# A two-layer decoder trunk on one core: evacuating transposes bank by bank, and holding weight splits back at three transitions

## The chip, the core and the metric

The kernel runs on one core of a Trainium2 chip. The engines named here are PE (matrix products and transposes), ACT and DVE (both read the accumulator memory PSUM as well as SBUF), POOL, and SP, which here issues the loads of weights. The metric is the device time of one execution in microseconds (us). A profiled execution gives its own time and, beside it, a span from the first to the last recorded instruction; the times quoted from the trace count from the start of the span.

## The reference

One sequence of 256 tokens with 1024 features passes two layers. Everything is float32.

```
h = h + stick_breaking_attention(rms_norm(h, g00), w_qkv, w_o)      # layer 0
h = h + sqrelu_mlp(rms_norm(h, g01), w1[0], w2[0])                  # (relu(x @ w1)^2) @ w2, width 4096
shared = nsa_shared_kv(h, kv_norm, w_kv, cmp_pos, cmp_w1, cmp_w2)   # K and V for three branches
h = h + nsa_attention(rms_norm(h, g10), w_q, gate_b, w_o, shared)   # layer 1: compressed, selected, window
h = h + sqrelu_mlp(rms_norm(h, g11), w1[1], w2[1])
return rms_norm(h, final_norm)
```

Both attentions have 16 heads of 64; in layer 1 three sigmoid gates per head weigh the branches.

## The kernel before

**Products.** A float32 operand is split into a rounded part (hi) and the rest (lo), and a product is taken as hi*hi + hi*lo + lo*hi (`mm3`; all matmuls stand in one helper, L346, all transposes in another, L358). A weight block of 128 x 2048 is loaded by SP into one of three buffers `raw` (L260), in two halves cast by ACT into `wh` (L292) and subtracted by DVE into `wl` (L298); `wh` and `wl` have three buffers too. When the second half's subtraction has been written down, the `raw` buffer is asked for again (`fetch`), which puts the next load on SP.

**Turning the tokens.** `hres` holds the residual stream of two token tiles (128 tokens each). Before an MLP and before layer 1's projections it is transposed: eight chunks of 128 features, four at a time. `xt_tr` puts four chunks into two PSUM banks, two to a bank (eight transposes, tile `pt`), and `xt_evac` takes each out: ACT scales it by the norm's gain (hi, L416), DVE multiplies again and subtracts hi (lo, L417). The results are called `xn` before an MLP and `xk` or `xq` in layer 1. Of the chunks, `2j + b` lies in bank `b` at place `j`: neighbouring chunks lie in different banks. The first four go ahead of the residual's last half, which is added meanwhile (L441 behind attention, L443 behind an MLP), the next four follow.

**Three transitions.** At the end of layer 0 and of layer 1 the output projection (`acc<-wh,oT`) ends, the residual is added, and the MLP's first matmuls (`pu<-xn,wh`) begin; between the first MLP and layer 1 the same happens in `to_nsa`, with `pk<-wh,xk` behind it. DVE and ACT split the following blocks' weights at the same time.

**Layer 1's attention.** For each pair of heads the scores become probabilities `pe` (exponential on ACT, L1058; row sums and gates `rs`; a multiply on DVE, L1086, or POOL, L1085). `turn(p, i, bank)` transposes a third of a pair's `pe` into a bank (tile `ptp`), and ACT or DVE copies it to `pT` (L1111). `values(g, bank)` multiplies by V into a bank (tile `po`), and `part(n, k)` adds a chunk of the output projection (tile `acc`).

**What sets the order.** The instructions of each engine are written out in a fixed order when the program is built, by a planner (`Order`). PE's order is the order of the code. The work of ACT, DVE and POOL stands in chains with a rank, and at each planned moment the free engine takes the ready instruction of the lowest rank; where a form for two engines exists, the one that is free takes it. Residual adds have rank 0.2, evacuations 0.5, splits of the block that PE is at 0.5, of the next block 2, of later ones 4. When PE comes to need a chain, its rank is set to 0. `quiet(engines, ns)` keeps an engine from taking work of rank 2 and above for a planned time. The planner's costs are estimates that only set the order; on the chip each engine takes its list in order and waits where it must.

Of the kernel before, what the change touches and what calls it, by code (L numbers as in the profile page):

```python
# [17 lines left out]
T = 2  # L18
# [153 lines left out]
def hybrid_kernel(ctx, tc, x, xt, eye, gcols, gfin, wqk, wv, wo0, wkv, wvs, wq, wg, wo1, w1, w2, cw1, cw2, cpos, gate_b, consts, out):  # L172
# [10 lines left out]
    def go(gen, rank=1, lag=LAG):  # L183
        return Chain(o, gen, rank, o.now + lag)
# [172 lines left out]
    def tr(o_, a, i, rate=2.0):  # L357
        nc.tensor.transpose(o_, a, i)  # L358
        o.tick(a.shape[0] / 2.4 * rate + 3)
# [42 lines left out]
    def xt_banks(banks):  # L402
        return [B(banks[b], f"pt{b}").rearrange("p (j q) -> p j q", j=2) for b in range(2)]

    def xt_tr(pt, half, ts=range(T)):
        for b in range(2):
            for j in range(2):
                k = 4 * half + 2 * j + b
                for t in ts:
                    tr(pt[b][:, j, t * P:(t + 1) * P], hres[t][:, k * P:(k + 1) * P], ident)  # L410

    def xt_evac(pt, half, gi, xt_, rank=0.5):
        def one(j, b):
            k = 4 * half + 2 * j + b
            g = gc[:, gi * NK + k:gi * NK + k + 1]
            yield act(256, lambda: nc.scalar.activation(xt_[0][:, k, :], pt[b][:, j, :], AF.Copy, scale=g), 60)  # L416
            yield dve(256, lambda: nc.vector.scalar_tensor_tensor(  # L417
                xt_[1][:, k, :], pt[b][:, j, :], g, f32(xt_[0][:, k, :]), op0=OP.mult, op1=OP.subtract), 60)
        return [go(one(j, b), rank) for j in range(2) for b in range(2)]

    def x_tiles(i, tag):
        xp = wide_slot(i, [P, NK, 2, T * P], F32R, f"x{tag}")
# [32 lines left out]
    def mlp(layer, gi, x_, ch, pt, rs, pus, accs, mid, ap):  # L455

        wa, wb = i_m[layer]
        acc = [[None, None], [None, None]]
        held = []
        r2 = [None, None]  # L460

        def second(c, hT, order, hook=None):
            for i, (t, n) in enumerate(order):
                for f in range(2):
                    w = W(wb[c], f)
                    if i == 0 and f == 0:
                        o.need(hT[2])
                    if c == 0 and f == 0:
                        acc[n][t] = B(accs[2 * n + t], f"acc{t}{n}")
                    mm3(acc[n][t], tok(hT, f, t), cut(w, f * D + n * 512, f * D + (n + 1) * 512),  # L470
                        c == 0 and f == 0, c == NFC - 1 and f == 1)
                if hook is not None:
                    hook(i, t, n)
            gone(wb[c])

        by_n = [(t, n) for n in range(2) for t in range(T)]
        by_t = [(t, n) for t in range(T) for n in range(2)]

        def begin(c):
            return ([B(pus[c % 2][f], f"pu{f}") for f in range(2)],  # L480
                    [ap.tile([P, 512], F32, name=m) for m in ("mr", "mu", "ms")], [])

        def first(c, st, f, k0, k1):
            pu, (r, u, s), chains = st
            for part in range(2):
                for k in range(k0, k1):
                    w = W(wa[c], k // 4)
                    if c < 2 and part == 0:
                        o.need(ch[k])
                    a = cut(w, k * 256 + f * P, k * 256 + (f + 1) * P)  # L490
                    if part == 0:
                        mm(pu[f], a[0], x_[2][:, k, :, :], k == 0, False)
                    else:
                        mm(pu[f][:, 0:T * P], a[1], x_[0][:, k, :], False, k == NK - 1)
            if k1 == NK:
                q = slice(f * 256, (f + 1) * 256)

                def gen():
                    yield act(256, lambda: nc.scalar.copy(r[:, q], pu[f][:, 256:512]))  # L499
                    yield dve(256, lambda: nc.vector.tensor_add(u[:, q], pu[f][:, 0:256], r[:, q]))  # L500
                chains.append(go(gen(), 0.4))

        def square(st):
            r, u, s = st[1]
            hh = ap.tile([P, 2, T * P], F32R, name="hh", bufs=3)
            hl = ap.tile([P, 2, T * P], F32R, name="hl", bufs=3)
            sv = s.rearrange("p (f q) -> p f q", f=2)

            def gen():
                for c in st[2]:  # L510
                    yield c
                yield dve(512, lambda: nc.vector.scalar_tensor_tensor(s, u, 0.0, u, op0=OP.max, op1=OP.mult), port=True)  # L512
                yield act(512, lambda: nc.scalar.copy(hh, sv))  # L513
                yield dve(512, lambda: nc.vector.tensor_sub(hl, sv, f32(hh)), port=True)  # L514
            return hh, hl, go(gen(), 0.4)

        st = [begin(0)]
        for f in range(2):
            first(0, st[0], f, 0, NK // 2)
        o.need(*rs)  # L520
        xt_tr(pt, 1)
        ch.extend(xt_evac(pt, 1, gi, x_))
        st.append(begin(1))
        for f in range(2):
            first(1, st[1], f, 0, NK // 2)
        for c in range(2):
            for f in range(2):
                first(c, st[c], f, NK // 2, NK)
            gone(wa[c])
            held.append((c, square(st[c])))  # L530
        for c in range(2, NFC):
            if c in (5, 7):
                go(inverse_of((c - 5) // 2, r2), 3)
            st = begin(c)
            for f in range(2):
                first(c, st, f, 0, NK)
            gone(wa[c])
            held.append((c, square(st)))
            second(*held.pop(0), by_n)
        second(*held.pop(0), by_n)  # L540

        def hook(i, t, n):
            mid(i, go(res(n, t, acc[n][t], r2[t]), 0.2))

        second(*held.pop(0), by_t if layer else by_n, hook)
# [3 lines left out]
    def layer0(ap):  # L549
# [209 lines left out]
        out_part(oT, acc, i_o0, 0, (6, 7), oc[3:4])  # L759
        gone(i_o0[1][0])  # L760
        rs = [go(res(0, t, acc[0][t]), 0.2) for t in range(T)]
        out_part(oT, acc, i_o0, 1, (5,))
        out_part(oT, acc, i_o0, 1, (6,), ts=(0,))
        x1 = x_tiles(0, "n")
        pt = xt_banks((6, 7))
        o.need(*rs)
        xt_tr(pt, 0)
        ch = xt_evac(pt, 0, 1, x1)
        out_part(oT, acc, i_o0, 1, (6,), ts=(1,))
        out_part(oT, acc, i_o0, 1, (7,), ts=(0,))  # L770
        rs = [go(res(1, 0, acc[1][0]), 0.2)]
# [7 lines left out]
    def layer1(xk, pt0, ch, ap):  # L779
# [63 lines left out]
        def kv_proj(n, banks, mid=None):  # L843
            pk = [B(b, "pk") for b in banks]
            for k in range(NK):
                if k == 4 and mid is not None:
                    mid()
                if n == 0 and k == 2:
                    o.need(nxt[2], nxt[3])
                    pt1 = xt_banks((6, 7))  # L850
                    xt_tr(pt1, 1)
                    ch.extend(xt_evac(pt1, 1, 4, xk))
                    rc.extend([go(rstd_of(t, rstd), 0.8) for t in range(T)])
                    for half in range(2):
                        for c, x in enumerate(xt_evac((pt0, pt1)[half], half, 2, xq, 2.5)):
                            qc[4 * half + c] = x
                w = W(i_kv[n][k // 4], k % 4 // 2)
                if n == 0:
                    o.need(ch[k])
                for t in range(T):  # L860
                    mm3(pk[t], tok(xk, k, t), cut(w, k % 4 * 512, (k % 4 + 1) * 512), k == 0, k == NK - 1)
                if k % 4 == 3:
                    gone(i_kv[n][k // 4])
            o.need(*rc)
            for t in range(T):
                if n == 0:
                    kd0c.append(go(first_out(t, pk[t])))
                else:
                    krope[t] = go(key_out(t, pk[t]), 0.9)
# [377 lines left out]
        def part(n, *ks):  # L1247
            out_part(oT, acc, i_o1, n, ks, [oc[k // 2] for k in ks])
# [51 lines left out]
        turn(3, 0, 2)  # L1300
        q_proj(3, 7, 4, 6)
        pcc[0].append(cmp_probs(0, cmp["s0"], 0))
        turn(3, 1, 2)
        q_proj(3, 7, 6, NK)
        turn(3, 2, 1)
        oT = o_tiles(0)
        oc = [None] * NG
        oc[0] = values(0, 0)
# [11 lines left out]
        pcc[1].append(cmp_probs(1, cmp["s1"], 2))  # L1320
        part(0, 2)
        turn(5, 0, 7)
        part(0, 3)
        gone(i_o1[0][0])
        turn(5, 1, 2)
        turn(5, 2, 7)
        oc[2] = values(2, 2)
        scores(7, Z)
# [14 lines left out]
        part(0, 6, 7)  # L1343
        gone(i_o1[1][0])
        rs = [go(res(0, t, acc[0][t]), 0.2) for t in range(T)]
        out_part(oT, acc, i_o1, 1, (6,), ts=(0,))
        x1 = x_tiles(1, "n")
        pt = xt_banks((6, 7))
        o.need(*rs)
        xt_tr(pt, 0)  # L1350
        ch1 = xt_evac(pt, 0, 3, x1)
        out_part(oT, acc, i_o1, 1, (6,), ts=(1,))
        out_part(oT, acc, i_o1, 1, (7,), ts=(0,))
        rs = [go(res(1, 0, acc[1][0]), 0.2)]
# [11 lines left out]

    def to_nsa(i, c):
        nxt[i] = c
        if i == 2:
            nxt["x"] = x_tiles(1, "k")  # L1370
            nxt["pt"] = xt_banks((4, 5))
            o.need(nxt[0], nxt[1])
            xt_tr(nxt["pt"], 0)
            nxt["ch"] = xt_evac(nxt["pt"], 0, 4, nxt["x"])

    scoped(mlp, "m0", 0, 1, x1, ch, pt, rs, ((4, 5), (6, 7)), (0, 1, 2, 3), to_nsa)
    x1, ch, pt, rs = scoped(layer1, "l1", nxt["x"], nxt["pt"], nxt["ch"], bufs=1)
# [128 lines left out]
```

## Time and profile before

| | |
|---|---|
| three runs | 627.76 us median (626.85 to 629.86) |
| profiled execution | 626.71 us, span 624.9 us, TensorE clock granted 0.997 |
| PE busy | 611.7 us, 98% of the span |
| DVE, ACT, POOL busy | 424.4, 328.9, 43.6 us |
| DMA | 108.23 MB, mean 173 GB/s |
| splits on DVE (`wl`, L298) | 192 times, 227.6 us |
| casts on ACT (`wh`, L292) | 192 times, 193.3 us |

The three transitions lie at about 111 to 124 us, 290 to 304 us and 433 to 447 us, layer 1's attention between the second and the third. In the page, a group or a row names the line, the engine, the operation and `out<-in`; an idle time before it is put in brackets with the instruction that ended it. Matmul starts follow each other closer than their lengths, since they are pipelined.

### The profile page before, as it was taken

Reading aid. Unit: us, or ns where it says so; the run is one execution under the profiler, and the core shown is the slowest. Engines: PE = TensorE matmul, PEld = TensorE weight load, DVE = VectorE, ACT = ScalarE, POOL = GpSimd, SP = SyncE. Lnnn points to the kernel's source line nnn. Section 1 sums busy time; section 2 is a strip of 40 time slices with the busy share of each in tenths; the row PEclk is TensorE's granted clock in tenths of the full one; section 3 lists DMA queues with packets and bytes.
Section 4 is the critical chain, followed back from the end, with each engine's and each line's share of the span. In section 5 each row is a group of like instructions: output and inputs, shape, how many; then the busy total and the mean of one; then the engine's idle time right before and its main releaser. Section 6 shows DMA issues by size and latency. Waiting matters only on the chain.

```text
span 624.9 us, 8905 instructions
## 1 busy us (share of the span) xinstructions
PE 611.7 (98%) x3570; PEld 514.2 (82%) x3570; DVE 424.4 (68%) x606; ACT 328.9 (53%) x556; POOL 43.6 (7%) x58
## 2 busy tenths in 40 slices
PE   9999999999999999999999999999999999999995
PEld 6898998788888888887887788677788888888884
DVE  6678896676656666556848999874676665566654
ACT  4756675464545444553815776454554554444432
POOL 0000000000000000000111552330000000000000
PEclk9999999999999999999999999999999999999998
DMA  8964324435554545554455353111455556455501
GB/s 295 393 244 165 113 93 182 149 138 205 194 211 166 195 181 199 202 192 164 174 201 202 137 201 136 69 68 68 168 209 199 200 180 215 162 193 193 203 1 67
DMA packets 17323, 108.23 MB, mean 173 GB/s; under 512 B 2305, under 2 KB 3073, under 8 KB 4993
## 3 DMA queue, kind: packets, MB, share of 16 engines
q1 hardware_dynamic: 16848, 107.11, 47.3%
q8 instruction: 28, 0.46, 0.3%
q10 hardware_dynamic: 432, 0.55, 0.2%
q14 instruction: 15, 0.11, 0.0%
HBM read 106.60 MB, written 1.05 MB: 172 GB/s over the span
## 4 chain that ended last, share of the span: by engine, by line
PE 82%; DVE 10%; DMA 2%; ACT 2%; issue 2%; SPq 0%; POOL 0%; POOLq 0%; ACTq 0%; DVEq 0%
PE acc L346 32%; PE pu L346 28%; PE qk L346 7%; DVE wl L298 4%; PE pk L346 3%; PE po L346 3%; PE z L346 2%; PE pv L346 2%; ACT wh L292 1%; DVE nm L1064 1%; DMA raw<-in_wq 1%; PE qp L346 1%; PE ph L346 1%; DMA raw<-in_wv 1%; PE pa L358 1%
## 5 line engine op out<-in xcount | busy, mean ns | idle before, releaser
L298 DVE TENSOR_TENSOR wl<-raw,wh 128x1024 fp32r<-128x1024 f32 (+1 forms) x192 | 227.6, 1206 | 109.8 <-ACT wh L292 107.4
L292 ACT CAST wh<-raw 128x1024 fp32r<-128x1024 f32 (+1 forms) x192 | 193.3, 1031 | 127.8 <-PE acc L346 54.3
L346 PE MATMUL pu<-xn,wh 128*128 128x512 f32 x512 | 130.1, 392 | 2.0 <-DVE xn L417 1.9
L346 PEld LDWEIGHTS pu<-xn,wh 128*128 128x128 f32 x512 | 93.3, 188 | 20.9 <-DVE xn L417 2.6
L346 PE MATMUL acc<-wh,hh 128*128 128x512 f32 x256 | 100.0, 391 | 0.0
L346 PE MATMUL acc<-wl,hh 128*128 128x512 f32 x256 | 99.9, 390 | 0.0
L346 PE MATMUL acc<-wh,hl 128*128 128x512 f32 x256 | 99.6, 389 | 0.0
L346 PEld LDWEIGHTS pu<-xn,wl 128*128 128x128 f32 x512 | 70.9, 190 | 5.6
L346 PE MATMUL pu<-xn,wl 128*128 128x256 f32 x512 | 72.6, 282 | 0.0
L346 PEld LDWEIGHTS acc<-wh,hl 128*128 128x128 f32 x256 | 48.1, 188 | 10.2
L346 PEld LDWEIGHTS acc<-wh,hh 128*128 128x128 f32 x256 | 48.2, 188 | 9.2
L346 PEld LDWEIGHTS acc<-wl,hh 128*128 128x128 f32 x256 | 48.2, 188 | 8.9
L513 ACT CAST hh<-ms 128x512 fp32r<-128x512 f32 x32 | 19.9, 621 | 61.7 <-DVE ms L512 61.7
L346 PE MATMUL qk<-xa,wh 128*128 128x256 f32 x256 | 47.3, 286 | 0.0
L346 PE MATMUL acc<-wh,oT 128*128 128x512 f32 x128 | 43.6, 403 | 0.0
L346 PEld LDWEIGHTS qk<-xa,wh 128*128 128x128 f32 x256 | 39.8, 191 | 0.5 <-issue 0.3
L346 PE MATMUL qk<-xa,wl 128*128 128x256 f32 x128 | 36.2, 283 | 0.0
L499 ACT COPY mr<-pu 128x256 f32<-128x256 f32 x64 | 23.6, 368 | 22.5 <-PE pu L346 22.5
L514 DVE TENSOR_TENSOR hl<-ms,hh 128x512 fp32r<-128x512 f32 x32 | 22.1, 692 | 19.4 <-ACT hh L513 19.4
L346 PE MATMUL pk<-wh,xk 128*128 128x512 f32 (+1 forms) x128 | 33.6, 342 | 0.0
L1058 ACT ACTIVATE pe<-z,nm 128x256 f32<-128x256 f32 (+1 forms) x64 | 26.1, 429 | 11.6 <-DVE nm L1064 11.4
L500 DVE TENSOR_TENSOR mu<-pu,mr 128x256 f32<-128x256 f32 x64 | 26.6, 418 | 5.2 <-ACT mr L499 5.2
(173 smaller groups left out, 731.6 us busy)
## 6 DMA issues: line engine op xcount, KB each, us to landing
raw<-in_w SPq DMA_DIRECT2D x64, 1024.0 KB, 4.8
raw<-in_wqk SPq DMA_DIRECT2D x8, 1024.0 KB, 7.3
raw<-in_wo SPq DMA_DIRECT2D x8, 1024.0 KB, 4.8
raw<-in_wkv SPq DMA_DIRECT2D x4, 1024.0 KB, 4.8
raw<-in_cw SPq DMA_DIRECT2D x4, 1024.0 KB, 4.8
raw<-in_wq SPq DMA_DIRECT2D x4, 1024.0 KB, 5.1
raw<-in_wv SPq DMA_DIRECT2D x2, 1024.0 KB, 5.8
raw<-in_wvs SPq DMA_DIRECT2D x2, 1024.0 KB, 5.0
```

The costliest lines, as they stand in the source:

```text
L292: nc.scalar.copy(ws.made[j][0][:, r], ws.raws[j][:, r])
L298: nc.vector.tensor_sub(ws.made[j][1][:, r], ws.raws[j][:, r], f32(ws.made[j][0][:, r]))
L346: nc.tensor.matmul(o_, a, b, start=first, stop=last, skip_group_check=True)
L358: nc.tensor.transpose(o_, a, i)
L499: yield act(256, lambda: nc.scalar.copy(r[:, q], pu[f][:, 256:512]))
L500: yield dve(256, lambda: nc.vector.tensor_add(u[:, q], pu[f][:, 0:256], r[:, q]))
L513: yield act(512, lambda: nc.scalar.copy(hh, sv))
L514: yield dve(512, lambda: nc.vector.tensor_sub(hl, sv, f32(hh)), port=True)
L1058: return act(n, lambda: nc.scalar.activation(d, z, AF.Exp, bias=nm[:, i:i + 1], accum_out=rs[:, t, hd, b:b + 1]), 150)
L1064: yield dve(256 * (t + 1), lambda: nc.vector.tensor_reduce(nm[:, i:i + 2], z, axis=AX.X, op=OP.max, negate=True))
```

## The change

Three things are edited. First, transposing and evacuating become one function, `xt_turn`: neighbouring chunks now lie in the same bank (`2b + j`), and the evacuations of a bank are put to the planner as soon as its four transposes stand in PE's list. Second, `quiet` is called at three transitions: for DVE and ACT over a planned 4500 ns at both transitions from attention to MLP, and for DVE over 1500 ns at each of the three calls of `to_nsa` with `i` below 3. Third, in layer 1 two turns exchange their banks (`turn(3,1)` now 1, `turn(3,2)` now 2), and `turn(5,1,2)` stands ahead of `part(0,3)`.

```diff
-    def xt_tr(pt, half, ts=range(T)):
-        for b in range(2):
-            for j in range(2):
-                k = 4 * half + 2 * j + b
-                for t in ts:
-                    tr(pt[b][:, j, t * P:(t + 1) * P], hres[t][:, k * P:(k + 1) * P], ident)
-
-    def xt_evac(pt, half, gi, xt_, rank=0.5):
-        def one(j, b):
-            k = 4 * half + 2 * j + b
-            g = gc[:, gi * NK + k:gi * NK + k + 1]
+    def xt_evac(pt, j, b, half, gi, xt_, rank=0.5):
+        k = 4 * half + 2 * b + j
+        g = gc[:, gi * NK + k:gi * NK + k + 1]
+
+        def one():
             yield act(256, lambda: nc.scalar.activation(xt_[0][:, k, :], pt[b][:, j, :], AF.Copy, scale=g), 60)
             yield dve(256, lambda: nc.vector.scalar_tensor_tensor(
                 xt_[1][:, k, :], pt[b][:, j, :], g, f32(xt_[0][:, k, :]), op0=OP.mult, op1=OP.subtract), 60)
-        return [go(one(j, b), rank) for j in range(2) for b in range(2)]
+        return go(one(), rank)
+
+    def xt_turn(pt, half, gi, xt_):
+        ch = []
+        for b in range(2):
+            for j in range(2):
+                k = 4 * half + 2 * b + j
+                for t in range(T):
+                    tr(pt[b][:, j, t * P:(t + 1) * P], hres[t][:, k * P:(k + 1) * P], ident)
+            ch += [xt_evac(pt, j, b, half, gi, xt_) for j in range(2)]
+        return ch
...
         rs = [go(res(0, t, acc[0][t]), 0.2) for t in range(T)]
+        o.quiet("DA", 4500)
         out_part(oT, acc, i_o0, 1, (5,))
         out_part(oT, acc, i_o0, 1, (6,), ts=(0,))
         x1 = x_tiles(0, "n")
         pt = xt_banks((6, 7))
         o.need(*rs)
-        xt_tr(pt, 0)
-        ch = xt_evac(pt, 0, 1, x1)
+        ch = xt_turn(pt, 0, 1, x1)
...
-        turn(3, 1, 2)
+        turn(3, 1, 1)
         q_proj(3, 7, 6, NK)
-        turn(3, 2, 1)
+        turn(3, 2, 2)
...
         turn(5, 0, 7)
+        turn(5, 1, 2)
         part(0, 3)
         gone(i_o1[0][0])
-        turn(5, 1, 2)
         turn(5, 2, 7)
...
         rs = [go(res(0, t, acc[0][t]), 0.2) for t in range(T)]
+        o.quiet("DA", 4500)
         out_part(oT, acc, i_o1, 1, (6,), ts=(0,))
...
-        xt_tr(pt, 0)
-        ch1 = xt_evac(pt, 0, 3, x1)
+        ch1 = xt_turn(pt, 0, 3, x1)
...
     def to_nsa(i, c):
         nxt[i] = c
+        if i < 3:
+            o.quiet("D", 1500)
         if i == 2:
             nxt["x"] = x_tiles(1, "k")
             nxt["pt"] = xt_banks((4, 5))
             o.need(nxt[0], nxt[1])
-            xt_tr(nxt["pt"], 0)
-            nxt["ch"] = xt_evac(nxt["pt"], 0, 4, nxt["x"])
+            nxt["ch"] = xt_turn(nxt["pt"], 0, 4, nxt["x"])
```

In the lists of the engines this shows at three places most of all. The first is DVE at the end of layer 0, from the first residual adds to the last subtract of the turned tokens (a tile's number is its buffer). Before:

```order
L441 TENSOR_TENSOR hres_75<-acc_986,hres_75 128x512
L441 TENSOR_TENSOR hres_76<-acc_987,hres_76 128x512
L298 TENSOR_TENSOR wl<-raw,wh 128x1024 x2
L417 SCALAR_TENSOR_TENSOR xn<-pt_1161,gc,xn 128x256
L417 SCALAR_TENSOR_TENSOR xn<-pt_1162,gc,xn 128x256
L417 SCALAR_TENSOR_TENSOR xn<-pt_1161,gc,xn 128x256
L441 TENSOR_TENSOR hres_75<-acc_1021,hres_75 128x512
L441 TENSOR_TENSOR hres_76<-acc_1022,hres_76 128x512
L417 SCALAR_TENSOR_TENSOR xn<-pt_1162,gc,xn 128x256
L298 TENSOR_TENSOR wl<-raw,wh 128x1024 x2
```

And with the change:

```order
L445 TENSOR_TENSOR hres_75<-acc_986,hres_75 128x512
L445 TENSOR_TENSOR hres_76<-acc_987,hres_76 128x512
L411 SCALAR_TENSOR_TENSOR xn<-pt_1156,gc,xn 128x256 x2
L411 SCALAR_TENSOR_TENSOR xn<-pt_1157,gc,xn 128x256 x2
L445 TENSOR_TENSOR hres_75<-acc_1021,hres_75 128x512
L445 TENSOR_TENSOR hres_76<-acc_1022,hres_76 128x512
L298 TENSOR_TENSOR wl<-raw,wh 128x1024 x3
L411 SCALAR_TENSOR_TENSOR xn<-pt_1187,gc,xn 128x256 x2
L411 SCALAR_TENSOR_TENSOR xn<-pt_1188,gc,xn 128x256 x2
```

The two splits that stood ahead of the first four subtracts stand behind them and behind the residual adds, and three splits in a row, not two, now precede the second four.

The second is DVE at the end of layer 1. Before:

```order
L298 TENSOR_TENSOR wl<-raw,wh 128x1024 x2
L417 SCALAR_TENSOR_TENSOR xn<-pt_4065,gc,xn 128x256
L441 TENSOR_TENSOR hres_75<-acc_3952,hres_75 128x512
L417 SCALAR_TENSOR_TENSOR xn<-pt_4066,gc,xn 128x256
L441 TENSOR_TENSOR hres_76<-acc_3953,hres_76 128x512
L417 SCALAR_TENSOR_TENSOR xn<-pt_4065,gc,xn 128x256
L417 SCALAR_TENSOR_TENSOR xn<-pt_4066,gc,xn 128x256
L298 TENSOR_TENSOR wl<-raw,wh 128x1024 x2
L417 SCALAR_TENSOR_TENSOR xn<-pt_4096,gc,xn 128x256
```

And with the change:

```order
L411 SCALAR_TENSOR_TENSOR xn<-pt_4062,gc,xn 128x256 x2
L411 SCALAR_TENSOR_TENSOR xn<-pt_4063,gc,xn 128x256 x2
L445 TENSOR_TENSOR hres_75<-acc_3952,hres_75 128x512
L445 TENSOR_TENSOR hres_76<-acc_3953,hres_76 128x512
L298 TENSOR_TENSOR wl<-raw,wh 128x1024 x4
L411 SCALAR_TENSOR_TENSOR xn<-pt_4091,gc,xn 128x256 x2
L411 SCALAR_TENSOR_TENSOR xn<-pt_4092,gc,xn 128x256 x2
```

Here all four splits stand behind the first four subtracts and the adds, and ahead of the second four.

The third is ACT at the turns of the sixth pair of heads in layer 1, where `turn(5,1)` moved. Before:

```order
L1237 COPY pcT<-pct 120x256
L1058 ACTIVATE pe,rs<-z_3790,nm 128x256 x2
L1058 ACTIVATE pe,rs<-z_3791,nm 128x256 x2
L1058 ACTIVATE pe,rs<-z_3792,nm 128x128 x2
L1058 ACTIVATE pe,rs<-z_3793,nm 128x128 x2
L292 CAST wh<-raw 128x1024 x2
```

And with the change:

```order
L1240 COPY pcT<-pct 120x256
L1061 ACTIVATE pe,rs<-z_3790,nm 128x256 x2
L1061 ACTIVATE pe,rs<-z_3791,nm 128x256 x2
L1114 COPY pT<-ptp 128x512
L1061 ACTIVATE pe,rs<-z_3792,nm 128x128 x2
L1061 ACTIVATE pe,rs<-z_3793,nm 128x128 x2
L292 CAST wh<-raw 128x1024 x2
```

The copy of that turn moved from DVE, where two copies stood in a row, to ACT, between the exponentials. One multiply of `pe` by `rs` (128 x 2 x 256) moved the other way, from POOL to DVE. Between the first MLP and layer 1 the DVE list changes as at the end of layer 0: one split moves behind the residual adds, and three in a row precede the second half's subtracts.

More of the change, by code (lines that the diff above doesn't have):

```diff
@@ L520, in mlp @@
         o.need(*rs)
-        xt_tr(pt, 1)
-        ch.extend(xt_evac(pt, 1, gi, x_))
+        ch.extend(xt_turn(pt, 1, gi, x_))
         st.append(begin(1))
@@ L850, in kv_proj @@
                     pt1 = xt_banks((6, 7))
-                    xt_tr(pt1, 1)
-                    ch.extend(xt_evac(pt1, 1, 4, xk))
+                    ch.extend(xt_turn(pt1, 1, 4, xk))
                     rc.extend([go(rstd_of(t, rstd), 0.8) for t in range(T)])
                     for half in range(2):
-                        for c, x in enumerate(xt_evac((pt0, pt1)[half], half, 2, xq, 2.5)):
-                            qc[4 * half + c] = x
+                        for b in range(2):
+                            for j in range(2):
+                                qc[4 * half + 2 * b + j] = xt_evac((pt0, pt1)[half], j, b, half, 2, xq, 2.5)
                 w = W(i_kv[n][k // 4], k % 4 // 2)
```

## The prediction

> **What bounds the kernel now.** The page was read first, then the waits of PE, then the timelines of DVE, ACT and PE around each of PE's waits, then the windows of layer 1.
>
> ```profile
> PE 611.7 (98%) x3570; PEld 514.2 (82%) x3570; DVE 424.4 (68%) x606; ACT 328.9 (53%) x556; POOL 43.6 (7%) x58
> PE pu L346 <- DVE xn L417: 1.9, 3, 0.9
> ...
> PE ptp L358 <- ACT pT L1111: 0.9, 1, 0.9
> ...
> PE pt L358 <- DVE hres L443: 0.7, 1, 0.7
> PE po L346 <- DVE pT L1111: 0.3, 1, 0.3
> ```
>
> PE is busy 98% of the span, and nothing that the change does takes a matmul away. So it can gain only what PE stands idle: these four rows (us in total, times, longest), six waits and 3.8 us together, each at a place that the diff touches. I call them A (end of layer 0), B (first MLP to layer 1), C and D (turns of layer 1) and E (layer 1 to the second MLP); the pu row holds A once and E twice.
>
> **A: layer 0 to its MLP.** DVE, ACT, PE (start, length, instruction, count, idle before and its releaser):
>
> ```profile
> 113.44 2.36 DVE L298 TENSOR_TENSOR wl<-raw,wh 128x1024 fp32r<-128x1024 f32 x2 [0.39 <-ACT wh L292]
> 117.14 1.28 DVE L441 TENSOR_TENSOR hres<-acc,hres 128x512 f32<-128x512 f32 x2
> 118.33 0.47 DVE L417 SCALAR_TENSOR_TENSOR xn<-pt,gc,xn 128x256 fp32r<-128x256 f32 x1
> 114.83 0.91 ACT L416 ACTIVATE xn<-pt,gc 128x256 fp32r<-128x256 f32 x2 [0.47 <-PE pt L358]
> 116.23 0.87 ACT L416 ACTIVATE xn<-pt,gc 128x256 fp32r<-128x256 f32 x2 [0.49 <-DVE xn L417]
> 117.16 0.84 PE L346 MATMUL pu<-xn,wh 128*128 128x512 f32 x3
> 118.86 0.50 PE L346 MATMUL pu<-xn,wh 128*128 128x512 f32 x1 [0.86 <-DVE xn L417]
> 119.20 0.64 PE L346 MATMUL pu<-xn,wl 128*128 128x256 f32 x4
> 124.75 0.40 PE L346 MATMUL pu<-xn,wh 128*128 128x512 f32 x1
> ```
>
> The fourth chunk of xn is subtracted at 118.33, behind two splits and two residual adds, and PE's fourth pu matmul starts at 118.86. Three such matmuls take 0.84 us where one takes 0.40, so they follow at 0.22 to 0.23 us; the group after the four would have begun at 117.16 + 4 x 0.228 = 118.07 and begins at 119.20. **A loses 1.13 us.** After the change the splits stand behind, and the two scalings of a bank follow each other: ACT from 114.83 (it waited for PE there, which the change leaves) at 0.45 us each to 116.6; DVE waits for the second of a bank, so its subtracts start at about 115.8, 116.2, 116.7, 117.1, and the fourth is ready at 117.6, ahead of 117.16 + 3 x 0.228 = 117.84. The stall goes whole.
>
> What is late next: DVE then has the two adds (1.28 us, to 118.8), three splits now instead of two (2.36 / 2 = 1.18 each, to 122.3) and four subtracts of the second half at 0.40 each, the last ready at 123.9 or 124.0. PE reaches that half 1.13 us sooner than 124.75, at 123.62, and its fourth chunk at 124.3. That is a cover of 0.3 to 0.4 us, thin, but enough: +1.13, with 0.8 as the lower end if one split takes longer.
>
> The order of the two engines inside a bank deserves a look. ACT's third scaling waited 0.49 us for DVE's read of the same bank (row of 116.23). The Trainium skill (PSUM — Partial Sum Buffer, PSUM bank collisions raise a hardware error) says that two engines on one bank and quadrant must be kept apart, ScalarE and VectorE too, and this row agrees. By that rule the new numbering only moves the wait to DVE, whose first subtract of each bank starts one scaling later; were that uncovered at A and E, the sum below would be smaller by two scalings, about 0.9 us. In this trace it is covered: at 115.8 DVE is still 1.4 us ahead of PE's first pu matmul.
>
> **B: first MLP to layer 1.**
>
> ```profile
> 293.34 1.22 DVE L298 TENSOR_TENSOR wl<-raw,wh 128x1024 fp32r<-128x1024 f32 x1
> 294.47 1.41 DVE L443 SCALAR_TENSOR_TENSOR hres<-acc,r,hres 128x512 f32<-128x512 f32 x2
> 294.29 0.27 PE L358 MATMUL pt<-ident,hres 128*128 128x128 f32 x1
> 295.27 0.98 PE L358 MATMUL pt<-ident,hres 128*128 128x128 f32 x7 [0.71 <-DVE hres L443]
> 303.38 0.39 PE L346 MATMUL pk<-wl,xk 128*128 128x512 f32 x1
> ```
>
> The second transpose needs the residual add that stood behind one split. Seven transposes take 0.98 us where one takes 0.27, a step of 0.12, so the second should have begun at 294.41: **0.86 us is lost**. With the split held, the add starts near 293.34, is done by 294.1, and the loss goes. Behind it DVE has an add, four subtracts and an add as before, then three splits instead of two. Counted on with the lengths above, the first subtract of the second half is ready near 302.3; PE asks for it two matmuls behind the last row, about 303.84, less 0.86 that it gained: 302.98. Cover 0.6 us. +0.86, lower end 0.4.
>
> **C: turn(3,1) into the other bank.**
>
> ```profile
> 384.86 0.66 PE L358 MATMUL ptp<-ident,pe 128*128 128x128 f32 x4 [0.92 <-ACT pT L1111]
> 393.00 0.68 DVE L435 TENSOR_TENSOR oT<-po,oT 128x512 fp32r<-128x512 f32 x1
> 393.95 0.48 PE L346 MATMUL acc<-wh,oT 128*128 128x512 f32 x1
> 383.00:396.00 13.00, 12.02 (x102) 8.50 (x101) 12.72 (x23) 8.28 (x27) 5.39 (x3) 1.00 0.46 156
> ```
>
> PE's transposes wait 0.92 us for the copy out of bank 2 (some 1.0 to 1.1 with their start-up); bank 1 is free, so this wait goes. But the last row (length, then busy time of PE, PEld, DVE, ACT, POOL) has DVE at work for 12.72 of 13.00 us here. What it does is not shortened, so its oT subtract still ends at 393.68, and PE, which now needs it at 393.95, would only come to it early and wait: 0 to 1.0 us, at least 0.27 less what ACT and POOL shift. I take **0**. What A and B give does pass through, since DVE's work of this stretch is set off by PE's own progress earlier on; if it were not, that is the second rival.
>
> **D: turn(5,1) ahead of part(0,3).**
>
> ```profile
> 407.96 1.29 DVE L1111 COPY pT<-ptp 128x512 f32<-128x512 f32 x2
> 407.32 1.04 PE L358 MATMUL ptp<-ident,pe 128*128 128x128 f32 x8
> 408.71 1.52 PE L346 MATMUL po<-pT,vs 128*64 128x256 f32 x16 [0.34 <-DVE pT L1111]
> 413.06 0.69 DVE L435 TENSOR_TENSOR oT<-po,oT 128x512 fp32r<-128x512 f32 x1 [1.41 <-ACT oT L434]
> ```
>
> po is written into bank 2, which turn(5,1), the first four of the eight transposes, has just filled; its copy is the first of the two on DVE, and po waits 0.34 us for it (0.53 by the step of (1.04 - 0.27) / 7 = 0.11 from 407.32 on). Six matmuls earlier, the four transposes are done some 1.4 us sooner, and in the new order the copy stands on ACT, between its wide and its narrow exponentials, where I put it at 406.5 to 407.1, a microsecond ahead of po. In exchange DVE takes one multiply of pe by rs from POOL: 0.69 us if it goes like the subtract over 128x512 in the last row, and DVE idles 1.41 us before 413.06, which hides it. **+0.45**, from 0 (the copy on ACT late) to 0.53.
>
> **E: layer 1 to the second MLP.**
>
> ```profile
> 435.86 2.36 DVE L298 TENSOR_TENSOR wl<-raw,wh 128x1024 fp32r<-128x1024 f32 x2 [0.44 <-ACT wh L292]
> 438.13 0.48 DVE L417 SCALAR_TENSOR_TENSOR xn<-pt,gc,xn 128x256 fp32r<-128x256 f32 x1
> 436.67 1.56 ACT L416 ACTIVATE xn<-pt,gc 128x256 fp32r<-128x256 f32 x4
> 435.21 1.25 PE L358 MATMUL pt<-ident,hres 128*128 128x128 f32 x8
> 438.16 0.40 PE L346 MATMUL acc<-wh,oT 128*128 128x512 f32 x1
> 439.66 0.49 PE L346 MATMUL pu<-xn,wh 128*128 128x512 f32 x1 [0.49 <-DVE xn L417]
> 440.74 0.86 PE L346 MATMUL pu<-xn,wh 128*128 128x512 f32 x2 [0.59 <-DVE xn L417]
> 441.44 0.65 PE L346 MATMUL pu<-xn,wl 128*128 128x256 f32 x4
> 446.98 0.40 PE L346 MATMUL pu<-xn,wh 128*128 128x512 f32 x1
> ```
>
> Here all four chunks come late: the first subtract starts at 438.13, behind the splits. Unhindered, the group after the four would start at 438.16 + 5 x 0.228 = 439.30; it starts at 441.44, so **2.14 us are lost**. After: ACT's two casts go behind too, so its four scalings (1.56 us) start when the first bank's four transposes are done, half-way through the row of 435.21 and a little more, at about 436.1, and end near 437.7; the subtracts, each behind the second scaling of its bank, are ready at 437.4, 437.8, 438.2 and 438.6, each ahead of its matmul (438.39 to 439.07). All 2.14 go. Then comes the bill: two adds to 439.8, and now **four** splits before the second half, 4 x 1.15 (two take 2.36 where one takes 1.22), to 444.4; four subtracts, the last ready at 446.0. PE, 2.14 earlier than 446.98, asks for the fourth of these at 444.84 + 0.69 = 445.53: a new wait of about 0.5 us. **+1.65**, from 1.0 (one split more, or waits for casts) to 2.14.
>
> **Sum:** 1.13 + 0.86 + 0 + 0.45 + 1.65 = 4.1 us. The ends, 0.8 + 0.4 + 0 + 0 + 1.0 = 2.2 and 1.13 + 0.9 + 1.0 + 0.53 + 2.14 = 5.7. The profiled execution took 626.71 us and would take 622.6. The median of the three runs shown is 1.05 us above it; on its scale I predict **623.7**.
>
> **The held splits' loads.** A raw buffer is loaded anew once its split is done, so holding a split back delays an issue on SP.
>
> ```profile
> raw<-in_w SPq DMA_DIRECT2D x64, 1024.0 KB, 4.8
> 130.13 1.05 ACT L292 CAST wh<-raw 128x1024 fp32r<-128x1024 f32 x1 [0.27 <-ACT mr L499]
> ```
>
> At A the first pair ended at 113.44 + 2.36 = 115.8 and now ends near 121.0: 5.2 us later, landing 4.8 later at 125.8. The buffer loaded then is cast at 130.13, 129.0 after the shift. Cover 3.2 us, so I price it at nothing. At B the load also passes the small loads of layer 1 on SP, and at E the first pair ends at 442.1 instead of 438.2; both covers are larger.
>
> **The rivals.**
>
> 1. *C counts too*: the stretch of layer 1 is not DVE's after all. For it: PE is itself busy 12.02 of 13.00 us there. Against: oT ends only 0.27 us ahead of its matmul. 4.1 + 1.0 = 5.1 us: 622.7.
> 2. *Part of it is swallowed*: A and B (2.0 us) are given back in layer 1 where DVE is full, or the splits moved behind stall the second halves by one split each at A and E. Either leaves 4.1 - 2.0 to 2.3 = about 2 us: 625.7. For it: the covers of 0.3 and 0.6 us are thin. Against: PE sets off the work in layer 1.
> 3. *Slower: loads come late.* One mechanism, the 5.2 us later issue at A and 3.9 at E, decides from a delay above the cover of 3.2 us, for instance if the loads queue behind one another and take 8 us and not 4.8. Then PE waits for a cast in the MLP's first blocks, with three buffers nothing makes up for it, and each transition costs up to what it was held: 5.2 + 3.9 - 4.1 = 5 us net, 632.8. Against it: each load has landed in 4.8 us in the median of 64.
> 4. *The order does less than the code says*: if the splits were needed at once, the planner would pull them forward again and nothing would change, 627.8. Against it the new order on DVE, in which they do stand behind.
>
> **The numbers.** Forecast 0.50, rival 1 0.13, rival 2 0.25, rival 3 0.07, rival 4 0.05. A change of 0.5%, 3.1 us, is about what a measurement of this kernel can tell from none; the border lies at 624.6. The forecast's own range is 623.0 to 625.3, some 0.43 of its 0.50 below the border; with rival 1 that makes 0.56 faster. The rest of the forecast, rival 2 and rival 4 are the 0.37 within, rival 3 the 0.07 slower. The range, 621.9 to 626.9, takes the forecast, rivals 1 and 2, and the ends of the sum (627.76 - 5.7 and, nearly, - 2.2 with a run's scatter).
>
> **What would show it.** Right: in the waits of PE the rows for hres, ptp at turn(3,1) and po are gone, and pu<-xn keeps one wait of about 0.5 us, in the second half of E, in place of three; DVE shows three, three and four splits in a row at A, B and E. C is wrong as I have it if PE's wait before turn(3,1) goes and no new one appears before 396. Rival 2 shows as new waits of PE on xn, xk or oT; rival 3 as casts waiting for raw. The prediction is wrong if PE's waits together do not fall below 2.5 us, or if they do and the span does not follow.

## The result and the profile after

| | median | range | ratio to before, 95% interval |
|---|---|---|---|
| before, five runs | 628.35 us | 626.85 to 629.86 | |
| changed, four runs beside them | 622.73 us | 622.64 to 623.97 | 0.9916 [0.9892, 0.9939] |
| before, 23 runs beside the first experiments | 627.99 us | 626.97 to 629.92 | |
| changed, six runs beside those | 624.12 us | 622.75 to 624.94 | 0.9933 [0.9918, 0.9948] |

A fifth execution of the first set took 1016.4 us at a TensorE clock of 0.56 of full speed, and the profile of that set is of that execution; so the profile after is taken from the second set: 623.75 us, span 622.0 us, clock 0.998. The change is faster, by 5.6 us in the first comparison and 3.9 us in the second; both intervals lie below 1 and they overlap. Its waits of PE:

```profile
PE pv L346 <- ACT wh L292: 1.4, 3, 0.9
PE warm L346 <- DVE zero L371: 1.2, 1, 1.2
PE pa L358 <- ACT sbe L671: 0.9, 1, 0.9
PE acc L346 <- DVE oT L439: 0.7, 1, 0.7
PE ptp L358 <- DVE pT L1114: 0.2, 1, 0.2
```

The rows for `pu`, `pt`, `po` and for the copy ahead of `turn(3,1)` are gone. Three are new: `acc` on `oT` and, behind it, `ptp` on a copy of DVE, which together take the place of the wait at C, and `pv` on `wh`, which lies in the first 30 us of the program, where nothing was changed.

A, the end of layer 0 (DVE, ACT, PE, all about 1.0 us later than before because of those first microseconds):

```profile
116.68 1.66 DVE L411 SCALAR_TENSOR_TENSOR xn<-pt,gc,xn 128x256 fp32r<-128x256 f32 x4 [2.66 <-ACT xn L410]
118.25 1.28 DVE L445 TENSOR_TENSOR hres<-acc,hres 128x512 f32<-128x512 f32 x2
119.45 3.49 DVE L298 TENSOR_TENSOR wl<-raw,wh 128x1024 fp32r<-128x1024 f32 x3
115.81 1.57 ACT L410 ACTIVATE xn<-pt,gc 128x256 fp32r<-128x256 f32 x4 [6.19 <-PE pt L358]
118.13 1.07 PE L346 MATMUL pu<-xn,wh 128*128 128x512 f32 x4
119.04 0.64 PE L346 MATMUL pu<-xn,wl 128*128 128x256 f32 x4
```

Four scalings follow each other on ACT, four subtracts on DVE, and the group behind the first four matmuls of PE begins 119.04 - 118.13 = 0.91 us after the first of them. Before, it was 119.20 - 117.16 = 2.04. That is 1.13 us. DVE waits 2.66 us for ACT ahead of its subtracts: it is early now.

B, the first MLP to layer 1 (DVE, PE):

```profile
292.52 1.40 DVE L447 SCALAR_TENSOR_TENSOR hres<-acc,r,hres 128x512 f32<-128x512 f32 x2
294.14 1.03 PE L358 MATMUL pt<-ident,hres 128*128 128x128 f32 x8
```

No split stands between the two adds any more, and the eight transposes follow each other without the wait of 0.71 us behind the first.

E, the end of layer 1 (DVE, PE):

```profile
435.53 1.66 DVE L411 SCALAR_TENSOR_TENSOR xn<-pt,gc,xn 128x256 fp32r<-128x256 f32 x4 [1.56 <-ACT xn L410]
438.30 4.62 DVE L298 TENSOR_TENSOR wl<-raw,wh 128x1024 fp32r<-128x1024 f32 x4
442.84 1.65 DVE L411 SCALAR_TENSOR_TENSOR xn<-pt,gc,xn 128x256 fp32r<-128x256 f32 x4
436.72 0.40 PE L346 MATMUL acc<-wh,oT 128*128 128x512 f32 x1
437.86 0.64 PE L346 MATMUL pu<-xn,wl 128*128 128x256 f32 x4
443.42 1.69 PE L346 MATMUL pu<-xn,wh 128*128 128x512 f32 x4
```

The first half starts on time: from the last `acc` to the group behind the four, 437.86 - 436.72 = 1.14 us where it was 441.44 - 438.16 = 3.28. That is the 2.14 us. But the four of the second half spread over 1.69 us in place of 1.09: DVE's four splits (4.62 us) stand ahead of their subtracts, and 0.6 us is lost again. This loss has no row in the list of waits; only the starts show it.

To see each place apart from the scatter of whole runs, I cut the trace at fixed instructions. PE's list holds 3570 instructions in every kernel shown here, in the same order but for the moved turn, so the time from the start of the n-th (counted from 0) to the start of the m-th can be compared. Cuts: n = 117 (among the first matmuls of `qk`), A 707 to 819, B 1643 to 1726, C 2271 to 2391, D 2447 to 2510, E 2635 to 2723. The "rest" is everything else behind 117, up to the end of PE's last instruction; the first column runs from the start of PE's first.

| kernel (one profile each) | first 117 | A | B | C | D | E | rest | all behind 117 |
|---|---|---|---|---|---|---|---|---|
| before | 28.83 | 20.80 | 17.93 | 16.09 | 8.00 | 18.01 | 507.19 | 588.02 |
| changed | 29.81 | 19.67 | 17.04 | 16.11 | 7.58 | 16.49 | 507.18 | 584.07 |
| e1, holds alone | 31.11 | 20.44 | 17.08 | 16.11 | 8.00 | 16.70 | 507.18 | 585.51 |
| e2, banks alone | 29.51 | 20.62 | 17.93 | 16.12 | 8.00 | 18.02 | 507.19 | 587.88 |
| e3, turns alone | 30.77 | 20.80 | 17.93 | 16.11 | 7.59 | 17.99 | 507.21 | 587.63 |
| e4, holds of 7000 | 28.40 | 19.67 | 17.04 | 16.12 | 7.57 | 15.87 | 507.22 | 583.49 |
| e5, holds of 20000 | 29.06 | 21.32 | 17.04 | 16.12 | 7.60 | 17.55 | 510.51 | 590.14 |
| e6, two copies on ACT | 33.10 | 19.67 | 17.04 | 14.82 | 7.59 | 16.49 | 507.19 | 582.80 |
| e7, DVE kept free in C | 29.97 | 19.67 | 17.04 | 14.68 | 7.58 | 16.50 | 507.18 | 582.65 |
| e8, e4 and e7 | 31.37 | 19.67 | 17.04 | 14.66 | 7.58 | 15.90 | 507.16 | 582.01 |
| e9, e7 with the old banks | 31.00 | 19.67 | 17.04 | 15.80 | 7.58 | 16.50 | 507.18 | 583.77 |

Where an edit did not reach, the columns agree to 0.03 us from one kernel to the next, the long rest to 0.06 us. So the change is worth 588.02 - 584.07 = **3.95 us** in this view: A 1.13, B 0.89, C -0.02, D 0.42, E 1.52. Among these eleven profiles, all that scatters by microseconds without an edit is the first column.

### The profile page after: what moved, and what is told of

Read it like the earlier page. It is cut to its first block, busy times and chain, and to the rows that moved or that the text cites. A ratio compares the mean times of both kernels' runs of the same rounds, so it can differ in the third digit from the quotient of the medians.

```text
span 1014.6 us, 8921 instructions
## 1 busy us (share of the span) xinstructions
PE 1006.2 (99%) x3570; PEld 673.1 (66%) x3570; DVE 429.0 (42%) x606; ACT 333.4 (33%) x557; POOL 40.0 (4%) x57
## 4 chain that ended last, share of the span: by engine, by line
PE 99%; DMA 0%; issue 0%; ACT 0%; POOL 0%; POOLq 0%; SPq 0%; DVE 0%
PE acc L346 36%; PE pu L346 29%; PE qk L346 7%; PE pk L346 5%; PE pv L346 4%; PE qp L346 4%; PE z L346 3%; PE po L346 3%; PE ptp L358 2%; PE ph L346 1%; PE pt L358 1%; PE pa L358 1%; DMA raw<-in_wv 0%; PE gp L346 0%; PE ptk L358 0%
## 5 line engine op out<-in xcount | busy, mean ns | idle before, releaser
L346 PE MATMUL pu<-xn,wh 128*128 128x512 f32 x512 | 210.4, 577 | 0.0
L346 PE MATMUL acc<-wh,hl 128*128 128x512 f32 x256 | 147.5, 576 | 0.0
L346 PE MATMUL acc<-wh,hh 128*128 128x512 f32 x256 | 147.5, 576 | 0.0
L346 PE MATMUL acc<-wl,hh 128*128 128x512 f32 x256 | 147.3, 575 | 0.0
L346 PEld LDWEIGHTS pu<-xn,wl 128*128 128x128 f32 x512 | 103.0, 233 | 25.5 <-issue 11.9
L346 PE MATMUL pu<-xn,wl 128*128 128x256 f32 x512 | 112.4, 382 | 0.0
L346 PE MATMUL qk<-xa,wh 128*128 128x256 f32 x256 | 72.6, 384 | 0.0
L346 PE MATMUL acc<-wh,oT 128*128 128x512 f32 x128 | 65.8, 586 | 0.0
L346 PEld LDWEIGHTS acc<-wh,oT 128*128 128x128 f32 x128 | 27.8, 217 | 20.2 <-issue 11.9
L346 PEld LDWEIGHTS pk<-wh,xk 128*128 128x128 f32 x128 | 29.4, 246 | 11.4 <-issue 6.7
```

Of the source, the lines that this page charges most:

```text
L346: nc.tensor.matmul(o_, a, b, start=first, stop=last, skip_group_check=True)
```

## The experiments

### The parts apart: e1, e2, e3

e1 has the three `quiet` calls alone, on the kernel before:

```diff
         rs = [go(res(0, t, acc[0][t]), 0.2) for t in range(T)]
+        o.quiet("DA", 4500)
...
         nxt[i] = c
+        if i < 3:
+            o.quiet("D", 1500)
```

> Only the three holds of splits; old numbering of chunks, old turns. Theory: B gives its 0.86 us. At A the fourth subtract still stands behind two residual adds in DVE's list, so A gives 0 to 0.2; at E it does too, so of 2.14 us about 1 comes. Together about 1.9 us less than before (1.4 to 2.4). Rival (the holds alone carry the change, the numbering does nothing): 3.6 us less.

e2 has `xt_turn` alone (the changed kernel without the `quiet` calls, with the old turns):

```diff
-        o.quiet("DA", 4500)
...
-        if i < 3:
-            o.quiet("D", 1500)
...
-        turn(3, 1, 1)
+        turn(3, 1, 2)
...
-        turn(3, 2, 2)
+        turn(3, 2, 1)
...
-        turn(5, 1, 2)
         part(0, 3)
         gone(i_o1[0][0])
+        turn(5, 1, 2)
```

> Only the transposes and evacuations bank by bank; no holds, old turns. Theory: the splits still stand ahead of the subtracts at A, B and E and the fourth subtract behind the adds, so nothing is gained: 0 (within 0.4 us). Rival (the numbering frees ACT from waiting for DVE and so carries A and E by itself): 2 to 3 us less.

e3 has the two edits to layer 1's turns alone:

```diff
-        turn(3, 1, 2)
+        turn(3, 1, 1)
...
-        turn(3, 2, 1)
+        turn(3, 2, 2)
...
+        turn(5, 1, 2)
         part(0, 3)
         gone(i_o1[0][0])
-        turn(5, 1, 2)
```

> Only the two edits to layer 1's turns. Theory: D gives 0.45 us, C nothing, since DVE is full there and PE waits for oT in place of pT: 0.45 us less. Rival (C counts): 1.4 to 1.5 us less, and no new wait of PE between 383 and 396.

Measured, as ratio of the timed runs and as time behind n = 117: e1 0.9948 [0.9932, 0.9963], 2.51 us less; e2 0.9992 [0.9981, 1.0003], 0.14 us less; e3 1.0008 [0.9994, 1.0022], 0.39 us less, which whole runs cannot tell from nothing.

e2 and e3 came as my theory had them. e1 gave more than its 1.4 to 2.4 us: A 0.36 (0 to 0.2 expected), B 0.85, E 1.31 (about 1). DVE and PE of e1 at A:

```profile
117.62 1.51 DVE L417 SCALAR_TENSOR_TENSOR xn<-pt,gc,xn 128x256 fp32r<-128x256 f32 x3 [2.29 <-ACT xn L416]
119.05 1.29 DVE L441 TENSOR_TENSOR hres<-acc,hres 128x512 f32<-128x512 f32 x2
120.25 0.48 DVE L417 SCALAR_TENSOR_TENSOR xn<-pt,gc,xn 128x256 fp32r<-128x256 f32 x1
120.78 0.50 PE L346 MATMUL pu<-xn,wh 128*128 128x512 f32 x1 [0.50 <-DVE xn L417]
```

The fourth subtract still stands behind the two adds, as said; but with the splits gone the adds begin sooner, and the wait falls from 0.86 to 0.50 us in place of staying. At E the same: of the two waits in the list one is left (PE of e1).

```profile
439.25 0.40 PE L346 MATMUL acc<-wh,oT 128*128 128x512 f32 x1
440.85 0.50 PE L346 MATMUL pu<-xn,wh 128*128 128x512 f32 x1 [0.53 <-DVE xn L417]
441.19 0.64 PE L346 MATMUL pu<-xn,wl 128*128 128x256 f32 x4
```

From the last `acc` to the group behind the four are 1.94 us, 0.80 more than the 1.14 of the changed kernel. Of the 2.14 us, e1 thus still loses 0.80 in the first half and, since E as a whole is 1.31 us shorter, next to nothing in the second: PE comes to it later and is not kept waiting by the four splits. That I had missed.

So the parts are not a sum of independent gains. At A the banks alone give 0.18, the holds alone 0.36, both 1.13: each leaves the other's obstacle (splits, or adds) in front of the fourth chunk. At E the banks alone give nothing, the holds 1.31, both 1.52. B is the holds alone: 0.85 of 0.89.

### What is left at E, and how long to hold: e4, e5

e4 and e5 change one number at both places in the changed kernel, to 7000 in e4 and to 20000 in e5:

```diff
-        o.quiet("DA", 4500)
+        o.quiet("DA", 7000)
```

> The changed kernel with 7000 in place of 4500 at the two transitions from attention to MLP. In DVE's list one split instead of four then stands ahead of the second half's subtracts at E, two instead of three at A. Theory: the 0.6 us that PE still loses at E is DVE's four splits, so E gives 2.1 us against before in place of 1.5, A the same 1.13; 0.6 us less than the changed kernel. Rival (that rest is not the splits', but ACT's or the transposes'): E stays at 1.5.

> The changed kernel with 20000 in place of 4500: splits of rank 2 are held over the MLP's first blocks and come when PE needs them. Theory of late loads (my rival 3): with raw buffers freed some 5 to 10 us later again, the cover of 3.2 us is gone, casts wait for raw, and PE loses 3 to 15 us in the first blocks of both MLPs. Rival: the planner pulls each split forward in time, and A and E cost at most 1 us.

e4: ratio 0.9926 [0.9902, 0.9950]; E went from 16.49 to 15.87, 0.62 us, A stayed. DVE and PE of e4 at E:

```profile
436.92 1.22 DVE L298 TENSOR_TENSOR wl<-raw,wh 128x1024 fp32r<-128x1024 f32 x1
439.84 1.66 DVE L411 SCALAR_TENSOR_TENSOR xn<-pt,gc,xn 128x256 fp32r<-128x256 f32 x4 [1.71 <-ACT xn L410]
441.51 3.50 DVE L298 TENSOR_TENSOR wl<-raw,wh 128x1024 fp32r<-128x1024 f32 x3
443.42 1.09 PE L346 MATMUL pu<-xn,wh 128*128 128x512 f32 x4
```

One split ahead, three behind, and the four matmuls take 1.09 us again. The bill at E was the splits', and all of the 2.14 us is to be had.

e5: ratio 1.0014 [1.0001, 1.0027], so the whole gain is lost. Behind n = 117 it is 590.14 - 584.07 = 6.07 us slower than the changed kernel: A 1.65, E 1.06, the rest 3.33 (1.20 in each MLP, 0.93 in layer 1 between B and C). In the lists of waits of PE and ACT and the timelines of PE and SP:

```profile
PE pu L346 <- ACT wh L292: 3.2, 4, 1.1
ACT wh L292 <- DMA raw<-in_w: 3.0, 2, 2.3
122.26 1.20 PE L346 MATMUL pu<-xn,wh 128*128 128x512 f32 x4 [1.06 <-ACT wh L292]
125.80 18.30 SPq L260 DMA_DIRECT2D raw<-in_w  x5
131.80 2.42 PE L346 MATMUL pu<-xn,wh 128*128 128x512 f32 x8 [0.53 <-ACT wh L292]
139.24 1.06 ACT L292 CAST wh<-raw 128x1024 fp32r<-128x1024 f32 x1 [0.76 <-DMA raw<-in_w]
```

The size lies in the 3 to 15 us of the theory of late loads, but the mechanism is another one than it said: PE waits for casts that were themselves held (the wait at 122.26 comes ahead of the first delayed load, which is asked for at 125.80). Late loads follow: ACT waits 3.0 us for `raw` of the MLPs' weights, a wait that is not in the list of the changed kernel. But the first cast that waits for such a load starts at 139.24, behind PE's last wait in that MLP (131.80), and from there to layer 1 PE falls no further behind the changed kernel. In the second MLP the same order holds, with PE's last wait at 454.44 and ACT's first for a load ahead of 463.38. So what the MLPs lose goes to the held casts, and the late loads cost PE nothing there. The 0.93 us in layer 1 are waits of transposes for DVE (0.4 us for `pT`, 0.3 us for `pe`); how the longer hold leads to them was not followed.

### What bounds C: e6, e7, e9

In the changed kernel PE reaches the end of this stretch sooner and waits there (PE, DVE, POOL):

```profile
382.73 0.60 PE L358 MATMUL ptp<-ident,pe 128*128 128x128 f32 x4
392.71 0.50 PE L346 MATMUL acc<-wh,oT 128*128 128x512 f32 x1 [0.67 <-DVE oT L439]
388.64 3.41 DVE L298 TENSOR_TENSOR wl<-raw,wh 128x1024 fp32r<-128x1024 f32 x2
391.97 0.68 DVE L439 TENSOR_TENSOR oT<-po,oT 128x512 fp32r<-128x512 f32 x1
388.82 2.14 POOL L1022 TENSOR_TENSOR qw<-qw,rbc 128x512 f32<-128x512 f32 x1 [2.92 <-DVE qw L1021]
```

The transposes of `turn(3,1)` wait no more, and `acc` waits 0.67 us for `oT`, where before the transposes waited 0.92. If DVE sets the end, taking work from it must show. e6 lets two copies go to ACT only; e7 keeps DVE from the two splits. In both the planner also gives DVE multiplies that POOL had, one in e6 and two in e7.

e6:

```diff
-                    yield {"A": (590, lambda: nc.scalar.copy(d, pt), False), "D": (685, lambda: nc.vector.tensor_copy(d, pt), False)}
+                    ways = {"A": (590, lambda: nc.scalar.copy(d, pt), False), "D": (685, lambda: nc.vector.tensor_copy(d, pt), False)}
+                    yield {"A": ways["A"]} if p == 3 and i else ways
```

> The changed kernel, but the copies of turn(3,1) and turn(3,2) can only go to ACT (DVE loses two copies of 0.68 us; the planner then also gives DVE the multiply qw by rbc that POOL had). Theory (DVE full sets the end of this stretch): oT comes earlier, PE's new wait of 0.7 us for it goes, and the stretch from 382 to 398 is 0.5 to 0.9 us shorter. Rival (PE's wait there hangs on ACT, POOL or its own chain): no shorter, or longer.

e7:

```diff
+        o.quiet("D", 6000)
         oc[0] = values(0, 0)
         scores(5, Z)
```

> The changed kernel with DVE kept from rank 2 for a planned 6000 ns from values(0) in layer 1 on: the two splits that took 3.41 us ahead of the oT subtract move behind it (and DVE takes POOL's two multiplies qw and qm). Theory (DVE full): PE's wait for oT goes, the stretch from 382 to 398 is 0.5 to 0.9 us shorter unless the moved splits stall the next one. Rival: no shorter.

Both shorten C, by 16.11 - 14.82 = 1.29 us and 16.11 - 14.68 = 1.43 us, more than the 0.5 to 0.9 I gave: behind the wait for `oT` stood a second one, for `pT` (0.2 us in the list of the changed kernel), and both went, with gaps too small for a row. (In e7 the copy behind the second one now goes to ACT.) The whole runs: e6 0.9926 [0.9901, 0.9951], e7 0.9929 [0.9901, 0.9957]. DVE and PE of e7:

```profile
388.96 0.69 DVE L1023 TENSOR_TENSOR qw<-qw,rbc 128x512 f32<-128x512 f32 x1
389.69 0.69 DVE L1025 TENSOR_TENSOR qm<-qm,qw 128x512 f32<-128x512 f32 x1
390.30 0.68 DVE L439 TENSOR_TENSOR oT<-po,oT 128x512 fp32r<-128x512 f32 x1
390.89 1.22 DVE L298 TENSOR_TENSOR wl<-raw,wh 128x1024 fp32r<-128x1024 f32 x1
391.97 0.48 PE L346 MATMUL acc<-wh,oT 128*128 128x512 f32 x1
```

`oT` is ready a microsecond ahead of its matmul, even though DVE took on POOL's two multiplies, at 0.69 us each where POOL needed 2.14.

Was C's edit then worth anything? e9 is e7 with the old banks:

```diff
-        turn(3, 1, 1)
+        turn(3, 1, 2)
...
-        turn(3, 2, 2)
+        turn(3, 2, 1)
```

> The kernel of e7_quietc with turn(3,1) and turn(3,2) in their old banks (2 and 1). Theory (C's edit removes a wait of 1.1 us that only shows once DVE is no longer full): the stretch from 382 to 398 is 14.7 + 1.1 = 15.8 us. Rival (once DVE is relieved the banks do not matter): 14.7.

C measured 15.80 us: the old wait is back (this row of PE in e9), and it costs 15.80 - 14.68 = 1.12 us.

```profile
385.04 0.66 PE L358 MATMUL ptp<-ident,pe 128*128 128x128 f32 x4 [0.94 <-ACT pT L1114]
```

So the exchange of banks is worth 1.1 us once DVE has room, and nothing (16.09 against 16.11) where it is full.

### Both together: e8

e8 is the changed kernel with 7000 in place of 4500 and with the line of e7.

> The changed kernel with 7000 in place of 4500 at the two transitions and with DVE kept from rank 2 for 6000 ns from values(0) on. Theory: the two effects lie in different stretches and add: behind the first 30 us, 0.6 + 1.4 us less than the changed kernel, 6.0 less than before. Rival: one eats the other, 5.4 or less.

621.45 us (621.05 to 623.24), ratio 0.9891 [0.9873, 0.9909]: the fastest of the kernels measured. Behind n = 117 it is 588.02 - 582.01 = 6.01 us less than before, as the theory had it. PE's list of waits then holds nothing between the attention of layer 0 and the end:

```profile
PE pv L346 <- ACT wh L292: 2.6, 2, 1.7
PE warm L346 <- DVE zero L371: 1.2, 1, 1.2
PE pa L358 <- ACT sbe L671: 0.9, 1, 0.9
```

### The changed kernel again: e0

> The changed kernel once more, for a profile at full clock. Theory (my sum): PE's waits at A (1.13 us), B (0.86), D (0.45) are gone, E keeps one of about 0.5 us in the second half, C's wait is gone but PE waits about as long for oT or pT before 396: 4.1 us less than before. Rival (C counts too): no new wait of PE between 383 and 396, 5.1 us less. Rival (swallowed): new waits of together 2 us in the second halves or in layer 1.

4.1 us was forecast, the ratio 0.9933 of 627.99 us is 4.2 us, and the trace behind n = 117 gives 3.95. The rivals are out: a new wait did appear between 383 and 396, and nothing was swallowed in the second half of A or B.

## Why the prediction was right

Step by step, forecast against the cut trace:

| step | forecast | measured | |
|---|---|---|---|
| A | 1.13 | 1.13 | cover behind it 0.3 to 0.4 forecast, about 0.8 found |
| B | 0.86 | 0.89 | |
| C | 0 | -0.02 | DVE full; shown by e6, e7 and e9 |
| D | 0.45 | 0.42 | copy on ACT at 405.53 |
| E | 1.65 | 1.52 | 2.14 won, 0.62 lost again (0.5 forecast) |
| sum | 4.1 | 3.95 | |

- **What bounds the kernel.** Four rows of PE's list of waits named all that the change moved. A, B, D and the first half of E went in the size read from the starts of the matmuls, not from the list: the list has 0.86 us at A, the starts 1.13, since idle time is counted from the end of the third matmul, 0.16 us behind the point at which the fourth would have started (118.00 against 117.84), and since the stalled matmul takes 0.50 us and not 0.40.
- **C.** The step that looked most like a free microsecond in the list of waits was rightly put at nothing. The window in which DVE works 12.72 of 13.00 us decided it, though about 1.0 us of that work is a wait for POOL (last section). What I did not see is that the limit was in reach: holding two splits there (e7) gives 1.4 us.
- **E.** The bill for holding four splits was seen and a little undersized, 0.5 for 0.62; e4 shows it was the splits' and could have been avoided. The sign that I had named for it, one row of `pu` on `xn` of about 0.5 us, did not come: the loss is spread over four matmuls that each start a little late, and only their starts show it.
- **D's exchange.** The new row of DVE, the multiply of `pe` by `rs`, cost 0.69 us at 408.37, as taken, and no one waited.

```profile
405.53 0.59 ACT L1114 COPY pT<-ptp 128x512 f32<-128x512 f32 x1
408.37 0.69 DVE L1089 TENSOR_TENSOR pe<-pe,rs 128x512 f32<-128x512 f32 x1
407.25 1.52 PE L346 MATMUL po<-pT,vs 128*64 128x256 f32 x16
```

- **Late loads (rival 3).** In the changed kernel no cast of the MLPs waits for a load. At a longer hold the price is real, and e5 loses all; the point of turning lies between 7000 and 20000. But what I had named as the mechanism, loads, is not what costs PE there: the held casts themselves are.
- **The time.** 623.7 us was forecast; 622.73 and 624.12 us are the two medians. They lie 1.4 us apart with the same program, and in the last section profiles of these kernels differ by as much and more in the first 30 us alone, so that the closeness of either is partly luck. The 3.95 us rest on the cut trace and owe little to it.

## What to carry to other kernels

Where one engine is busy 98% of the time, read its stalls from the starts of its own instructions, and for each stall name the queue that is late; then ask what stands in that queue behind the thing you move, because that is late next (E's second half). A wait that ends when a saturated engine gets round to it is not removed by another buffer: relieve the engine first, and the buffer is then worth its full price (C: 0 alone, 1.1 us once DVE had room). Work that is held back should be let go again piece by piece, not all at once ahead of the next thing that is urgent, and not so late that it becomes urgent itself: holds of 4500, 7000 and 20000 gave 3.95, 4.53 and -2.12 us.

## What the runs showed of the hardware

**The scatter of the profiled executions sits in the first 30 us.** Over these eleven profiles, the time from PE's first instruction to n = 117 lies between 28.40 and 33.10 us, while the 507 us of untouched work behind it agree within 0.06 us (e5 apart, which changed it). In that time PE waits for casts of `wv`, and ACT for its loads. The DMA's total in the first 30 us goes with it; e4 (28.40 us), before (28.83), changed (29.81), e8 (31.37) and e6 (33.10), one row each of their DMA views:

```profile
DMA packets 2813, 10.40 MB, mean 347 GB/s; under 512 B 432, under 2 KB 944, under 8 KB 2096
DMA packets 2797, 10.26 MB, mean 342 GB/s; under 512 B 433, under 2 KB 945, under 8 KB 2097
DMA packets 2766, 10.04 MB, mean 335 GB/s; under 512 B 429, under 2 KB 941, under 8 KB 2093
DMA packets 2737, 9.82 MB, mean 327 GB/s; under 512 B 427, under 2 KB 939, under 8 KB 2091
DMA packets 2715, 9.68 MB, mean 323 GB/s; under 512 B 422, under 2 KB 934, under 8 KB 2086
```

In these five, the less has been moved, the later PE is. It is not strict over all eleven: e7, with 10.23 MB, comes at 29.97 us, behind e2 with 10.14 MB at 29.51. That the loads' pace causes it is argued from this tendency and from ACT's waits for `raw<-in_wv` (7.0 us before, 11.2 in e6), not shown by an experiment. It could in part run the other way, since later loads are asked for only when PE and the splits have come on: the loads of `wqk` behind the first are asked for from 18.96 us on in e4 and from 22.38 in e6. It is not the chip: e4 (28.40) and e6 (33.10) ran on the same one. Why the pace differs stays open.

**DVE and POOL take turns.** In C of the changed kernel, DVE's two splits take 3.41 us beside POOL's multiply of 2.14 us, and 1.21 to 1.22 us each when they do not wait for it (e6, e7). The Trainium skill (SBUF — State Buffer, SBUF: two separate sides) says that VectorE (DVE) with two SBUF inputs and GpSimd (POOL) share a pair of ports as an exclusive lock held for the whole instruction. The rows agree. Two of POOL's multiplies of the same size took 2.04 us where no split stood beside them (POOL, before):

```profile
396.93 2.04 POOL L1085 TENSOR_TENSOR pe<-pe,rs 128x512 f32<-128x512 f32 x2 [2.71 <-DVE rs L1075]
```

One split, then a multiply of about 1.0 us, then the other split make up 3.4 us. The same pair of splits took 3.42 us in the kernel before, so a busy DVE is not always a DVE at work. In e7, 3.41 us go from ahead of `oT` and two multiplies of 0.69 us come; about 1.0 us of the exchange is this wait. No run moves POOL's multiply alone, so its share in the gains of e6 and e7 is not shown.
